# Relative-position rows of the second block: written in eight pieces from 128 partitions, in the first feed-forward

## The chip, the core and the metric

One NeuronCore of one Trainium2 chip runs the whole program. The metric is the device time of one execution in microseconds (us), as the median of three runs. Engines are named PE (TensorE), ACT (ScalarE), DVE (VectorE), POOL (GpSimd) and SP (SyncE); SP does nothing here but issue transfers.

## What is computed

Two transformer blocks run one after the other on 256 tokens of width 2048, in float32. The first block has a gated convolution, an attention with forget gates and a feed-forward of width 8192; the second has an attention with a learned relative-position bias, a pooling branch and a gated feed-forward. All that concerns the change is the bias of the second attention:

```python
dist_own = q_pos[:, None] - (own * MOBA_BLOCK + offs)[None, :]
bias_own = rel_bias[:, rel_bucket(dist_own)].astype(jnp.float32)
s_own = jnp.where(dist_own >= 0, s_own + bias_own, NEG)
```

With 256 tokens there is one block, so only this own block counts. The bias of a head depends on the distance of query and key alone: one row of 383 values per head, for distances 255 down to -127 (NEG where negative), holds everything. Query t reads that row from a start that moves by one element per query.

## The kernel before, in words

**Weights.** All large products stream their weights once. A weight tile is 512 rows by (mostly) 512 columns, 1 MB, loaded by `fetch` (line 831) as one transfer that SP issues into one of four `raw` buffers. `split_unit` (line 840) splits half a tile, a *unit*, into a high part `wh` (ACT, line 846) and a remainder `wl` (DVE, line 847), each with four buffers. `both` (line 882) then runs one *step*: six matmuls (line 887) for one 128-row slice of the weights: `wh` twice and `wl` once for each half of the tokens. A unit is two steps, a tile is four, and a chunk of 512 output columns is up to four tiles, 16 steps. The main loop (line 898) emits for each unit the split of the unit three ahead, the fetch of the tile four ahead (in the second unit of a tile), and the two steps.

**Small work.** Everything else hangs in a heap of tasks with due times counted in steps. `later(delay, fn, keys)` puts one in; after each step up to three due tasks are emitted, in the order of due time and then of insertion; `need(key)` emits tasks until the key is there. `chain` puts several in, `gap` steps apart. The order of emission is the order on each engine's own queue. `before[chunk]` runs a function ahead of a chunk's first step, after the split of the unit three ahead.

**Order of the chunks.** Values of block one (three chunks, steps 0 to 47), then queries and keys in two halves (steps 48 to 111), convolution, gates, output, and from step 464 the first feed-forward `w_ff1`: chunk j=0 is steps 464 to 479, j=1 steps 480 to 495, j=2 starts at 496. Its results are evacuated by `evac_ff` (line 559), turned by DVE transposes (line 190) into `z_t`, and split into the `k_u` operands of `w_ff2`.

**The bias.** `rel_bias_rows` (line 629) is queued for step 40. It loads a one-hot table `oh` (33x384) and the bias `rb` (33x8) on POOL's queue. A task 18 steps later multiplies them on PE into `p_b` (8x384, line 638), copies that on DVE into `e` (8 partitions, line 640) and writes `e` to DRAM 128 times over, skewed by one element per copy: one POOL transfer `ed<-e` (line 642) with 8 heads, 128 copies and 383 elements, 1532 KB. `rel_bias_tiles` (line 647) reads it back in four transfers into two `k_nb` tiles when the second block's first half of keys is done, at about 1440 us. `oh` and `e` come from the pool `s` with two buffers, which `squares` and the heads' `s_att` also use; `p_b` from the PSUM pool `tr` with four.

**What else is near step 58.** `cumulated` (line 406) writes the forget gates' sums `cd` and reads them back into two `k_nb` tiles (lines 425 and 426) on POOL's queue, `masked` (line 429) adds a mask on DVE, and two `bg` rows for the gates (line 505) stand behind the `ed` write on POOL's queue; they are first used at 330 us.

Of the kernel before, what the change touches and what calls it, by code (L numbers as in the profile page):

```python
# [11 lines left out]
F32 = mybir.dt.float32  # L12
# [7 lines left out]
P = 128  # L20
# [3 lines left out]
NH = 8  # L24
# [5 lines left out]
CW = 512  # L30
# [31 lines left out]
def tile_two_blocks(  # L62
# [5 lines left out]
    nc = tc.nc  # L68
    V, S, TE = nc.vector, nc.scalar, nc.tensor

    def pool(name, bufs, space=None):
        kw = {"space": space} if space else {}
        return ctx.enter_context(tc.tile_pool(name=name, bufs=bufs, **kw))
# [7 lines left out]
    s_p = pool("s", 2)  # L81
    pt_p = pool("pt", 3)
    bg_p = pool("bg", 2)
    st_p = pool("st", 4)
    dr_p = pool("dr", 1, DRAM)
# [7 lines left out]
    def later(delay, fn, *keys):  # L93
        seq[0] += 1
        heapq.heappush(tasks, (now[0] + delay, seq[0], fn, keys))

    def chain(delay, stages, *keys, gap=1):

        for i, fn in enumerate(stages):
            later(delay + i * gap, fn, *(keys if i == len(stages) - 1 else ()))  # L100
# [11 lines left out]
    def need(*keys):  # L112
        for key in keys:
            while key not in ready:
                run_one()
# [19 lines left out]
    chunks, before = [], {}  # L135

    def add_chunk(w, row0s, c0, ncol, acts, evac):

        chunks.append((w, row0s, c0, ncol, acts, evac))
# [7 lines left out]
    def split_out(key, j, n, p, scales=None):  # L147

        if key not in K:
            kt_tile(key)  # L150
        hi, lo = (K[key][:, h, j:j + n, :] for h in range(2))

        def to_hi():
            if scales is None:
                S.copy(hi, p)
            else:
                for i in range(n):
                    S.activation(hi[:, i, :], p[:, i, :], AF.Copy, scale=scales[i])

        def to_lo():  # L160
            if scales is None:
                V.tensor_tensor(out=lo, in0=p, in1=hi.bitcast(F32), op=OP.subtract)  # L162
            else:
                for i in range(n):
                    V.scalar_tensor_tensor(out=lo[:, i, :], in0=p[:, i, :], scalar=scales[i],
                                           in1=hi[:, i, :].bitcast(F32), op0=OP.mult, op1=OP.subtract)
        return [to_hi, to_lo]
# [12 lines left out]
    def turned(z, use, delay, keys, rate=3, lag=1):  # L180

        t = {}

        def part(i0, i1):
            if i0 == 0:
                t["o"] = z_p.tile([P, 4, T], F32, tag="z", name="z_t")
            for q, j in [divmod(i, 4) for i in range(i0, i1)]:
                src = z[32 * q:32 * q + 32].rearrange("p b (k c) -> p b k c", c=P)[:, :, :, 32 * j:32 * j + 32]
                dst = t["o"][32 * j:32 * j + 32].rearrange("p k (b t) -> p b k t", b=TB)[:, :, :, 32 * q:32 * q + 32]
                V.transpose(dst, src)  # L190

        def rest():
            for b in range(2):
                chain(lag + b, use(b, t["o"][:, 2 * b:2 * b + 2, :]), *keys[2 * b:2 * b + 2])
        n = 0
        for i in range(0, 16, rate):
            later(delay + n, lambda i=i: part(i, min(i + rate, 16)))
            n += 1
        later(delay + n - 1, rest, keys[0] + " turned")

    def group_keys(key):
        return [f"{key} {j}" for j in range(4)]
# [100 lines left out]
    AT = {}  # L303
# [233 lines left out]
    def evac_add(n, then=None):  # L537
        def evac(acc, tb=None):
            if tb is not None:
                V.tensor_tensor(out=xs[n][:, tb, :], in0=xs[n][:, tb, :], in1=acc, op=OP.add)  # L540
                nc.sync.dma_start(outr[:, tb, n * CW:(n + 1) * CW], xs[n][:, tb, :])
                return
            V.tensor_tensor(out=xs[n], in0=xs[n], in1=acc, op=OP.add)  # L543
            if then:
                then(n)
        return evac
# [12 lines left out]
    def evac_ff(key):  # L559
        def evac(acc):  # L560
            z = z_p.tile([P, TB, CW], F32, tag="z", name="z_f")
            for tb in range(TB):
                S.activation(z[:, tb, :], acc[:, tb, :], AF.Relu, scale=R["r2"][:, tb:tb + 1])
            later(1, lambda: S.activation(z, z, AF.Square))
            turned(z, lambda b, p: split_out(key, 2 * b, 2, p), 2, group_keys(key))
        return evac
# [44 lines left out]
    def k2_done(half):  # L611
        def then(z):
            y = st_p.tile([P, 8], F32, tag="hy", name="hy")
            chain(0, headnorm(z, y), f"rk{half}", gap=1)

            def scaled():
                need(f"rk{half}")
                zz = z.rearrange("p b (h d) -> p (b h) d", d=P)
                V.tensor_tensor(out=zz, in0=zz, in1=y[:, :, None].to_broadcast([P, 8, P]), op=OP.mult)
            later(5, scaled)  # L620
            transposed(z, qk_use(2, half, 1, col("kn", 0)), 8, group_keys(f"2k{half}"))
            if half == 0:
                rel_bias_tiles()
            for i in range(4):
                h = 4 * half + i
                head_task(2, h, 12 + 7 * i)
        return then

    def rel_bias_rows():
        oh = s_p.tile([33, 384], F32, tag="s", name="oh")  # L630
        nc.gpsimd.dma_start(oh, cst[0:33, C_OH:C_OH + 384])
        rb = const.tile([33, NH], F32, name="rb")
        nc.gpsimd.memset(rb[32:33, :], 1.0)
        nc.gpsimd.dma_start(rb[0:32, :], rel_bias_2.rearrange("h b -> b h"))

        def task():
            p = tr_p.tile([P, 512], F32, tag="tr", name="p_b")
            TE.matmul(p[0:8, 0:384], rb, oh, start=True, stop=True)
            e = s_p.tile([NH, 384], F32, tag="s", name="e")
            V.tensor_copy(e, p[0:8, 0:384])  # L640
            ed = dr_p.tile([NH, P * CW], F32, name="ed")
            nc.gpsimd.dma_start(bass.AP(tensor=ed.tensor, offset=ed.offset, ap=[[P * CW, NH], [CW + 1, P], [1, 383]]),
                                e[:, None, 0:383].to_broadcast([NH, P, 383]))
            AT["ed"] = ed
        later(18, task, "ed")

    def rel_bias_tiles():
        need("ed")
        ed = AT["ed"]
        for half in range(2):  # L650
            nb = k_p.tile([P, 4, MAXCOL], F32, tag="k", name="k_nb")
            o = ed.offset + half * 4 * P * CW + 127
            for c0, o, n in ((0, o + P, P), (P, o, T)):
                nc.gpsimd.dma_start(nb[:, :, c0:c0 + n],
                                    bass.AP(tensor=ed.tensor, offset=o, ap=[[CW, P], [P * CW, 4], [1, n]]))
            AT[2, "nb", half] = nb

    def v2_done(half):
# [128 lines left out]
    for blk in range(4):  # L787
        for i in range(4):
            j = 4 * blk + i
            add_chunk(w_ff1[0], G4, j * CW, CW, hT("f"), evac_ff(f"u{j}"))  # L790
        for n in range(4):
            add_chunk(w_ff2[0], [(4 * blk + i) * CW for i in range(4)], n * CW, CW, [f"u{4 * blk + i}" for i in range(4)],
                      evac_add(n, close_block if blk == 3 else None))
# [17 lines left out]
    j = 0  # L811
# [65 lines left out]
        later(4 * n + 3, lambda n=n: squares(part0, n))  # L877
    later(16, first_rstd, "r1")
    later(18, load_vectors)
    later(40, rel_bias_rows)  # L880

    def both(k, kt, wh, wl, stop):

# [77 lines left out]
```

## Time and profile before

| what | value |
|---|---|
| median of 3 runs | 2411.72 us (2409.83 to 2412.51) |
| the profiled execution | 2411.87 us |
| its span, first to last instruction | 2410.1 us |
| PE busy | 2369.9 us, 98% of the span |
| DVE busy / ACT busy | 1662.6 us (69%) / 1158.9 us (48%) |
| mean granted clock of PE | 0.995 |
| moved by DMA | 456.67 MB, mean 189 GB/s |

The profiled execution lies 1.8 us above its span and 0.15 us above the median. An engine's busy share is a mean over the whole program. PE is so near to full that its gaps can be counted one by one, so the question to ask of any other engine or transfer is in which of these gaps it ended last.

### The profile page before, as it was taken

How to read it: one execution, taken by the hardware profiler on the slowest of the kernel's cores; microseconds unless marked ns; L12 is line 12 of the kernel's file. 1: busy time of each engine (PE TensorE's matmuls, PEld its weight loads, DVE VectorE, ACT ScalarE, POOL GpSimd, SP SyncE). 2: the span in 40 equal slices, each digit the busy share in tenths (PEclk: the TensorE clock that was granted, in tenths of full speed). 3: DMA queues.
4: the chain of work that ended last, by engine and by line, in shares of the span. 5: the costliest groups of instructions: out<-in, count | busy, mean ns of one | idle time of the engine just before them, and what ended most of it. 6: DMA issues, size and time to landing. Idle time of an engine off the chain costs nothing.

```text
span 2410.1 us, 27828 instructions
## 1 busy us (share of the span) xinstructions
PE 2369.9 (98%) x10649; PEld 1962.8 (81%) x10649; DVE 1662.6 (69%) x2293; ACT 1158.9 (48%) x1514; POOL 36.5 (2%) x53
## 2 busy tenths in 40 slices
PE   9899999999999999999999999999999999999999
PEld 9688888888888888888888887888778888888877
DVE  5487776666877567577477856667787467865884
ACT  5355444444454354354345446545555345544453
POOL 1000000000000000000000000000000000000000
PEclk9899999999999999999999999999999999999999
DMA  7755565655556556555555665555555555555554
GB/s 256 188 183 171 197 207 194 210 202 176 192 179 206 192 190 195 192 192 192 192 186 181 197 209 194 161 177 190 180 181 193 192 185 182 188 194 185 185 175 140
DMA packets 230966, 456.67 MB, mean 189 GB/s; under 512 B 8085, under 2 KB 15997, under 8 KB 230832
## 3 DMA queue, kind: packets, MB, share of 16 engines
q1 hardware_dynamic: 227584, 445.81, 56.4%
q0 software_dynamic: 3248, 9.08, 1.6%
q8 instruction: 83, 1.36, 0.2%
q14 instruction: 51, 0.42, 0.0%
HBM read 451.18 MB, written 3.67 MB: 189 GB/s over the span
## 4 chain that ended last, share of the span: by engine, by line
PE 88%; DVE 6%; ACT 3%; DMA 2%; issue 1%; SPq 0%; ACTq 0%
PE acc L887 85%; DVE wl L847 2%; DVE z_t L190 2%; ACT wh L846 2%; DMA raw<-in_w_in_dram 2%; DVE z_cv L484 1%; PE p_t L175 1%; ACT z L440 1%; PE acc_last L887 0%; ACT z_cv L479 0%; PE p_t L360 0%; PE p_s L316 0%; PE p_t L714 0%; PE p_p L351 0%; DVE x L543 0%
## 5 line engine op out<-in xcount | busy, mean ns | idle before, releaser
L847 DVE TENSOR_TENSOR wl<-raw,wh 128x1024 fp32r<-128x1024 f32 (+1 forms) x848 | 1022.1, 1214 | 653.1 <-ACT wh L846 565.2
L846 ACT CAST wh<-raw 128x1024 fp32r<-128x1024 f32 (+1 forms) x848 | 874.9, 1042 | 726.3 <-PE acc L887 671.0
L887 PE MATMUL acc<-wh,k_g 128*128 128x512 f32 x1408 | 379.3, 391 | 0.0
L887 PE MATMUL acc<-wh,k_h 128*128 128x512 f32 (+1 forms) x1344 | 352.5, 384 | 12.7 <-ACT wh L846 12.7
L887 PEld LDWEIGHTS acc<-wh,k_g 128*128 128x128 f32 x1408 | 263.6, 188 | 53.9
L887 PEld LDWEIGHTS acc<-wh,k_h 128*128 128x128 f32 x1344 | 248.5, 189 | 58.5 <-ACT wh L846 14.0
L887 PE MATMUL acc<-wh,k_u 128*128 128x512 f32 x1024 | 274.8, 389 | 4.5 <-DVE k_u L162 4.5
L887 PE MATMUL acc<-wh,k_f 128*128 128x512 f32 x1024 | 273.9, 389 | 0.0
L887 PEld LDWEIGHTS acc<-wh,k_u 128*128 128x128 f32 x1024 | 191.9, 188 | 45.8 <-DVE k_u L162 6.2
L887 PEld LDWEIGHTS acc<-wh,k_f 128*128 128x128 f32 x1024 | 192.1, 188 | 39.7
L887 PE MATMUL acc<-wl,k_g 128*128 128x512 f32 x704 | 217.5, 390 | 0.0
L887 PE MATMUL acc<-wl,k_h 128*128 128x512 f32 (+1 forms) x672 | 201.4, 381 | 0.0
L887 PE MATMUL acc<-wh,k_d 128*128 128x512 f32 x656 | 176.9, 392 | 0.0
L887 PE MATMUL acc<-wl,k_f 128*128 128x512 f32 x512 | 157.6, 389 | 0.0
L887 PE MATMUL acc<-wl,k_u 128*128 128x512 f32 x512 | 157.6, 389 | 0.0
L887 PEld LDWEIGHTS acc<-wl,k_g 128*128 128x128 f32 x704 | 132.6, 188 | 27.9
L190 DVE STREAM_TRANSPOSE z_t<-z 32x256 f32<-32x256 f32 x336 | 146.4, 436 | 5.6
L887 PEld LDWEIGHTS acc<-wl,k_h 128*128 128x128 f32 x672 | 125.4, 189 | 23.2 <-DVE wl L847 0.3
L887 PEld LDWEIGHTS acc<-wh,k_d 128*128 128x128 f32 x656 | 123.2, 189 | 25.2
L887 PE MATMUL acc<-wh,k_i 128*128 128x512 f32 x512 | 140.0, 395 | 0.0
L190 DVE STREAM_TRANSPOSE z_t<-z_f 32x256 f32<-32x256 f32 x256 | 111.5, 436 | 4.1
L887 PEld LDWEIGHTS acc<-wl,k_f 128*128 128x128 f32 x512 | 96.1, 188 | 20.0
(227 smaller groups left out, 2010.3 us busy)
## 6 DMA issues: line engine op xcount, KB each, us to landing
raw<-in_w_ff_dram SPq DMA_DIRECT2D x128, 1024.0 KB, 5.2
raw<-in_w_in_dram SPq DMA_DIRECT2D x104, 1024.0 KB, 5.1
raw<-in_w_up_dram SPq DMA_DIRECT2D x88, 1024.0 KB, 5.0
raw<-in_w_down_dram SPq DMA_DIRECT2D x44, 1024.0 KB, 5.1
raw<-in_w_mix_out_dram SPq DMA_DIRECT2D x16, 1024.0 KB, 5.1
raw<-in_w_out_dram SPq DMA_DIRECT2D x16, 1024.0 KB, 5.1
raw<-in_w_conv_out_dram SPq DMA_DIRECT2D x8, 1024.0 KB, 5.3
raw<-in_w_attn_out_dram SPq DMA_DIRECT2D x8, 1024.0 KB, 5.5
```

The lines of the kernel that those rows point to most:

```text
L175: TE.transpose(p[:, j, tb * P:(tb + 1) * P], z[:, tb, (2 * b + j) * P:(2 * b + j + 1) * P], ident)
L190: V.transpose(dst, src)
L440: S.activation(z[:, tb, :], acc[:, tb, :], AF.Copy, scale=R[rname][:, tb:tb + 1])
L484: V.scalar_tensor_tensor(out=o[:, i, d:T], in0=u[:, i, 0:T - d], scalar=w(i, 2 - d), in1=o[:, i, d:T], op0=OP.mult, op1=OP.add)
L846: S.copy(wh[:, :, 0:ncol], raw)
L847: V.tensor_tensor(out=wl[:, :, 0:ncol], in0=raw, in1=wh[:, :, 0:ncol].bitcast(F32), op=OP.subtract)
L887: TE.matmul(halves[tb][:, 0:ncol], k[:, i, kt, tb * P:(tb + 1) * P], w[:, kk, 0:ncol], start=begin and first and kt == 0, stop=end and stop)
```

## The change

`rel_bias_rows` no longer runs at step 40 but ahead of the second chunk of the first feed-forward (step 480); its task follows 18 steps later. There, DVE first repeats each column of `rb` 16 times into a new tile `rbw` (33x128), so that the same matmul gives 128 rows instead of 8: 16 copies of each head's row. `e` then has 128 partitions. The one transfer on POOL's queue becomes eight on SP's, 20 steps apart from step 500 to step 640; each takes all 128 partitions and writes 128 rows of 383 elements. A head's area in DRAM is 513 elements per row in place of 512, and the addresses of the reads follow it.

```diff
-        later(18, task, "ed")
+            rbw = st_p.tile([33, NH, per], F32, tag="rbw", name="rbw", bufs=1)
+            V.tensor_copy(rbw, rb[:, :, None].to_broadcast([33, NH, per]))
             p = tr_p.tile([P, 512], F32, tag="tr", name="p_b")
-            TE.matmul(p[0:8, 0:384], rb, oh, start=True, stop=True)
-            e = s_p.tile([NH, 384], F32, tag="s", name="e")
-            V.tensor_copy(e, p[0:8, 0:384])
-            ed = dr_p.tile([NH, P * CW], F32, name="ed")
-            nc.gpsimd.dma_start(bass.AP(tensor=ed.tensor, offset=ed.offset, ap=[[P * CW, NH], [CW + 1, P], [1, 383]]),
-                                e[:, None, 0:383].to_broadcast([NH, P, 383]))
-            AT["ed"] = ed
+            TE.matmul(p[:, 0:384], rbw.rearrange("b h i -> b (h i)"), oh, start=True, stop=True)
+            e = s_p.tile([P, 384], F32, tag="s", name="e")
+            V.tensor_copy(e, p[:, 0:384])
+            ed = AT["ed"] = dr_p.tile([NH, P * ROW], F32, name="ed")
+
+            def write(k):
+                nc.sync.dma_start(bass.AP(tensor=ed.tensor, offset=ed.offset + k * ROW, ap=[[NH * ROW, P], [1, 383]]),
+                                    e[:, 0:383])
+            chain(2, [lambda k=k: write(k) for k in range(P // per)], "ed", gap=20)
+        later(18, task)
...
+            if j == 1:
+                before[len(chunks)] = rel_bias_rows
             add_chunk(w_ff1[0], G4, j * CW, CW, hT("f"), evac_ff(f"u{j}"))
...
     later(18, load_vectors)
-    later(40, rel_bias_rows)
```

`per` is 16 (128 rows over 8 heads) and `ROW` is 513; `rel_bias_tiles` uses `P * ROW` where it had `P * CW` for the stride between heads.

## Rows read from the trace of the kernel before

**Rows 1.** The page: busy time, share of the span and instructions by engine.
```profile
PE 2369.9 (98%) x10649; PEld 1962.8 (81%) x10649; DVE 1662.6 (69%) x2293; ACT 1158.9 (48%) x1514; POOL 36.5 (2%) x53
```
**Rows 2.** Who waited for whom, 70 to 140 us: total, times, longest us.
```profile
ACT k_qk L372 <- DVE z_t L190: 13.9, 2, 8.1
ACT wh L846 <- DMA raw<-in_w_in_dram: 13.7, 2, 13.0
PE acc L887 <- ACT wh L846: 11.2, 1, 11.2
```
**Rows 3.** Timeline of PE, 84 to 136 us: start, us, instruction, idle before it.
```profile
101.40 1.07 PE L887 MATMUL acc<-wh,k_h 128*128 128x512 f32 x4
...
102.76 1.07 PE L887 MATMUL acc<-wh,k_h 128*128 128x512 f32 x4
...
104.27 1.08 PE L887 MATMUL acc<-wh,k_h 128*128 128x512 f32 x4
...
116.98 2.08 PE L887 MATMUL acc<-wh,k_h 128*128 128x512 f32 x4 [11.17 <-ACT wh L846]
...
119.70 1.91 PE L887 MATMUL acc<-wh,k_h 128*128 128x512 f32 x4
...
121.93 1.09 PE L887 MATMUL acc<-wh,k_h 128*128 128x512 f32 x4
...
123.32 1.07 PE L887 MATMUL acc<-wh,k_h 128*128 128x512 f32 x4
```
**Rows 4.** Windows: length, busy by engine, granted clock (PEclk), DMA share, GB/s.
```profile
81.00:105.00 24.00, 24.00 (x107) 19.67 (x106) 16.74 (x26) 8.26 (x10) 0.00 (x0) 1.00 0.76 140
105.00:117.00 12.00, 0.83 (x5) 0.37 (x3) 0.04 (x1) 1.12 (x2) 0.00 (x0) 0.62 0.61 152
670.00:760.00 90.00, 90.00 (x398) 74.55 (x398) 69.20 (x102) 44.20 (x50) 0.00 (x0) 1.00 0.60 195
```
**Rows 5.** DMA issues, whole span: tile, queue, count, KB each, us to landing.
```profile
raw<-in_w_ff_dram SPq DMA_DIRECT2D x128, 1024.0 KB, 5.2
ed<-e POOLq DMA_DIRECT2D x1, 1532.0 KB, 37.7
out_dram<-x SPq DMA_DIRECT2D x2, 256.0 KB, 2.0
```
**Rows 6.** Timelines of POOL and SP, 60 to 140 us: when transfers were issued.
```profile
76.37 1.11 POOL L642 DMA_DIRECT2D ed<-e  x1 [2.49 <-DVE e L640]
...
80.36 0.37 SPq L837 DMA_DIRECT2D raw<-in_w_in_dram  x1
```
**Rows 7.** DMA issues in windows of 80, 95 and 125 us: that fetch, later ones.
```profile
raw<-in_w_in_dram SPq DMA_DIRECT2D x1, 1024.0 KB, 35.4
...
raw<-in_w_in_dram SPq DMA_DIRECT2D x1, 1024.0 KB, 24.7
...
raw<-in_w_in_dram SPq DMA_DIRECT2D x1, 1024.0 KB, 5.0
```
**Rows 8.** Timeline of ACT, 84 to 124 us.
```profile
102.29 0.62 ACT L372 COPY k_qk<-z_t 128x512 f32<-128x512 f32 x1
115.88 1.99 ACT L846 CAST wh<-raw 128x1024 fp32r<-128x1024 f32 x2 [12.97 <-DMA raw<-in_w_in_dram]
```
**Rows 9.** Timeline of PE, 72 to 80 us: the small matmul between two steps.
```profile
74.68 0.81 PE L638 MATMUL p_b<-oh,rb 33*8 33x384 f32 x2
```
**Rows 10.** Timelines of PE and DVE, 703 to 712 us: around step 498.
```profile
704.74 1.07 PE L887 MATMUL acc<-wh,k_f 128*128 128x512 f32 x4
...
706.10 1.07 PE L887 MATMUL acc<-wh,k_f 128*128 128x512 f32 x4
...
705.82 1.23 DVE L847 TENSOR_TENSOR wl<-raw,wh 128x1024 fp32r<-128x1024 f32 x1 [2.14 <-PE acc L887]
706.96 1.32 DVE L190 STREAM_TRANSPOSE z_t<-z_f 32x256 f32<-32x256 f32 x3
```
**Rows 11.** Groups of DVE copies by form: count, busy us, mean ns, idle before.
```profile
L640 DVE COPY e<-p_b 8x384 f32<-8x384 f32 x1 | 0.5, 545 | 1.6 <-PE p_b L638 1.6
...
L285 DVE COPY vcol<-p_v 128x160 f32<-128x160 f32 x1 | 0.3, 326 | 1.2 <-PE p_v L284 1.2
...
L412 DVE COPY c<-p_c 128x16 f32<-128x16 f32 x1 | 0.2, 168 | 0.0
```
**Rows 12.** Timelines of SP and ACT, 704 to 732 us.
```profile
707.07 0.37 SPq L837 DMA_DIRECT2D raw<-in_w_ff_dram  x1
...
722.21 1.06 ACT L846 CAST wh<-raw 128x1024 fp32r<-128x1024 f32 x1 [0.23 <-ACT wh L846]
```

More of the change, by code (lines that the diff above doesn't have):

```diff
@@ L627, in k2_done @@
         return then
+    ROW = CW + 1
     def rel_bias_rows():
@@ L634, in rel_bias_rows @@
         nc.gpsimd.dma_start(rb[0:32, :], rel_bias_2.rearrange("h b -> b h"))
+        per = P // NH
         def task():
+            rbw = st_p.tile([33, NH, per], F32, tag="rbw", name="rbw", bufs=1)
+            V.tensor_copy(rbw, rb[:, :, None].to_broadcast([33, NH, per]))
             p = tr_p.tile([P, 512], F32, tag="tr", name="p_b")
-            TE.matmul(p[0:8, 0:384], rb, oh, start=True, stop=True)
-            e = s_p.tile([NH, 384], F32, tag="s", name="e")
-            V.tensor_copy(e, p[0:8, 0:384])
-            ed = dr_p.tile([NH, P * CW], F32, name="ed")
-            nc.gpsimd.dma_start(bass.AP(tensor=ed.tensor, offset=ed.offset, ap=[[P * CW, NH], [CW + 1, P], [1, 383]]),
-                                e[:, None, 0:383].to_broadcast([NH, P, 383]))
-            AT["ed"] = ed
-        later(18, task, "ed")
+            TE.matmul(p[:, 0:384], rbw.rearrange("b h i -> b (h i)"), oh, start=True, stop=True)
[7 more added lines that the diff above has]
+        later(18, task)
     def rel_bias_tiles():
@@ L651, in rel_bias_tiles @@
             nb = k_p.tile([P, 4, MAXCOL], F32, tag="k", name="k_nb")
-            o = ed.offset + half * 4 * P * CW + 127
+            o = ed.offset + half * 4 * P * ROW + 127
             for c0, o, n in ((0, o + P, P), (P, o, T)):
                 nc.gpsimd.dma_start(nb[:, :, c0:c0 + n],
-                                    bass.AP(tensor=ed.tensor, offset=o, ap=[[CW, P], [P * CW, 4], [1, n]]))
+                                    bass.AP(tensor=ed.tensor, offset=o, ap=[[CW, P], [P * ROW, 4], [1, n]]))
             AT[2, "nb", half] = nb
```

## Prediction

> **What bounds the kernel now.** I read the page's busy times first: PE works for 98% of the span [rows 1], so what a change can win is a gap of PE or work of PE. Next come the waits and, where they are longest, PE's timeline. The waits between 70 and 140 us hold one large gap: PE stood 11.2 us for ACT's `wh`, and ACT stood 13.0 us for a weight fetch [rows 2]. In PE's timeline a step of six matmuls starts every 1.36 us (101.40 to 102.76). The next starts are 104.27, 116.98, 119.70, 121.93 and 123.32 [rows 3], so the intervals exceed 1.36 us by 0.15, 11.35, 1.36, 0.87 and 0.03: 13.76 us lost in one place. The last part of that is the clock. The granted clock was 1.00 up to 105 us and 0.62 on average in the 12 us of the gap, and the first matmuls after it ran at half pace, 2.08 us for four against 1.07 [rows 3, 4].
>
> Why the fetch was late is in the transfers. `ed<-e` was issued at 76.37 us and took 37.7 us, so it landed at 114.1 [rows 5, 6]. The fetch issued at 80.36 took 35.4 us and landed at 115.8, just when ACT resumed (115.88) [rows 6 to 8]; one issued at 96.36 still took 24.7 us, and one after `ed` had landed took 5.0 [rows 7]. A usual fetch takes 5.2 us [rows 5]. Meanwhile the DMA engines were busy 0.76 of the time at only 140 GB/s, against 0.60 at 195 in the first feed-forward [rows 4]. The skewed write held engines with slow packets, and the weights queued with it.
>
> **What the change removes.** The write leaves this place. What is late next? ACT was itself behind: it waited 8.1 us for the turned `z_t` [rows 2], and finished the second `k_qk` copy at 102.29 + 0.62 = 102.9 us [rows 8]. Without the late fetch (80.36 + 5.2 = 85.6, and even three times as slow still 96) the next `wh` runs 102.9 to 103.95 and `wl` by about 105.2. PE wants `wh` when the step that began at 104.27 ends, 105.6, and `wl` about 0.9 us later. So the unit comes in time by about a microsecond. No further transposes are due before the chunk's end, so the next splits follow at about 1.2 us each against 2.72 us of PE per unit, and the lead grows. I keep the 0.15 us before the gap as DVE's and take 13.6 us as the gain; bounds are 13.76, and 13.6 less one whole unit (2.7) if ACT and DVE come that much later than I read.
>
> PE, DVE and POOL also lose `p_b`, `e` and the issue here, and get them back at step 498. On PE the two small matmuls took 0.81 us [rows 9]; with 384 columns in both forms I take the same duration for 128 output rows, plus about 0.1 us for a wider weight load, so this move is worth +0.1 us.
>
> **What it adds on PE.** At step 498 the matmul now stands directly behind a DVE copy emitted at the same place, which the old matmul did not: it was fed by loads 18 steps old. PE would come to it at 706.10, between the second and third step of the chunk. DVE at that point is in `wl` of the unit three ahead, 705.82 to about 706.96, when its next instruction starts [rows 10]. The copy `rbw` has 128 elements on 33 partitions. Between 168 ns for 16 elements and 326 for 160 [rows 11] this is 168 + 158 x 112/144 = 0.29 us, an estimate. PE therefore waits from 706.1 to 707.3: **+1.2 us**. Bounds: 0 if `wl` runs a microsecond earlier, 2.5 if the three transposes (1.32 us) come first; by insertion order they do not. Behind the waiting matmul stand all later steps, so this is paid in full. DVE then waits for the matmul and copies `e` (128 partitions and 384 elements, 545 ns as with 8 partitions [rows 11]); its transposes and splits move by 0.3 + 0.8 + 0.5 = 1.6 us, less than PE's own 1.2 + 0.9, so nothing else becomes late.
>
> **What it adds on SP and the DMA engines.** Eight issues of 0.37 us, as one of a fetch takes [rows 6], on a queue that waits most of the time. The first one waits for `e`, until about 708.6; the fetch of 707.07 stands behind it and goes out at about 709, 2 us late, where PE is 2.1 us late too. That fetch is first needed at about 722.2 [rows 12], 15 us after its issue, and takes 5.2: a cushion of 10 us. Each piece is 191.5 KB. From below, a 256 KB store from 128 partitions landed in 2.0 us; from above, an eighth of the old write is 37.7 / 8 = 4.7 us [rows 5]. Twenty steps are 27 us with five fetches in them, at a DMA share of 0.60 [rows 4], so even 4.7 us falls in free time, and a fetch behind a piece is at most 4.7 us late, under half of the cushion. I take 0 us on the path. If the cushion were gone, it would be 2.0 to 4.7 us a piece. The store is the nearer row, since it too leaves from 128 partitions. POOL's loads of `oh` and `rb` move to step 480, 18 steps (24 us) ahead of use as before. The `s` buffer that `e` holds for 140 steps is not asked for meanwhile: nothing in the feed-forward's first half uses that pool. The read-back at 1440 us follows step 640 by some 500 us.
>
> The Trainium skill speaks against the split ("DMA: Bandwidth & Descriptors", Rules for kernel authors): transfers should be joined into 1 MiB or more, because each pays a fixed part of about 2.0 us. By that page's fit a piece would be an estimated 2.45 us and the eight 19.6 us, and paid on the path they would turn the sum into a loss of about 7 us. The trace agrees on the size (2.0 us for 256 KB) but shows such stores beside work, so I keep the rule for a rival.
>
> **The sum.** 2411.87 (profiled) - 13.6 + 1.2 + 0.1 = 2399.6; less 0.15 for the distance to the median, **2399.4 us**, a gain of 12.3 us or 0.5%.
>
> **The rivals.**
> *The gap shrinks but does not close.* The forget gates' reads and the late `z_t` remain, and with them ACT's lateness. For it: ACT's 8.1 us wait [rows 2] is no DMA's fault. Against: the next unit's sources are in place at 102.9, 2.7 us before PE runs dry. Losing one to three units' time of the gain gives 2402 to 2407, say 2404.
> *Nothing is won.* The fetches were slow for another reason (the bias rows and `k_nb` reads queued around the same time), or the time is given back later. Against: fetches recover at the moment `ed` lands, and PE at 98% has no later wait that an earlier start would lengthen. About 2412.
> *Slower: the pieces stand in the weights' way.* All eight go on SP's queue ahead of fetches. If their time is paid in line instead of hidden, 8 x 2.0 = 16 us by the store's row: 2399.4 + 16 = 2415.4; at 4.7 us each, 2437. It begins when a piece delays the following fetch by more than the 10 us cushion. Against: that is five times the store and twice an eighth of the old write. This is also where the page's rule leads.
>
> **How the numbers follow.** Forecast 0.86, shrunken gap 0.07, nothing won 0.04, slower 0.03. The forecast's own range: from 2411.7 - 13.76 + 0.1 = 2398.1 (PE waits not at all) to 2411.7 - 10.9 + 2.5 + 0.1 = 2403.4, each end with about 1 us for the spread of the runs (2.7 us from lowest to highest); the upper end lies in the rival's reach already. So 2397 to 2404. A measurement of this kernel can tell about 0.2%, 4.8 us, from no change: faster 0.92, within it 0.05, slower 0.03.
>
> **What would show it.** Right: no gap of PE over a microsecond between 80 and 130 us, granted clock 1.00 there, fetches issued after 76 us landing in 5 to 8 us; near 693 us (12 to 14 us earlier than now) one wait of PE for DVE's `rbw` of about 1.2 us; eight stores of 191.5 KB in 2 to 5 us with no wait of ACT for `raw` from 680 to 900 us. Wrong: a wait of `wh` for `raw` behind any store, a lasting PE gap near 105 us that ends with `z_t` or `k_qk`, or a second fall of the clock.

## The result

| | before | after |
|---|---|---|
| median, us | 2410.97 (2409.83 to 2412.51, 4 runs) | 2398.68 (2397.03 to 2401.46, 4 runs) |
| ratio, 95% interval | | 0.995 (0.9939 to 0.9962) |
| profiled execution, span | 2411.87, 2410.1 | 2401.46, 2399.7 |

The change saves 12.3 us, 0.5%; the 95% interval runs from 0.4% to 0.6%. The profiled execution of after is the slowest of its four runs, so the two traces differ by 10.4 us and not by 12.3. From the page of after:

```profile
PE 2369.0 (99%) x10649; PEld 1962.4 (82%) x10649; DVE 1662.5 (69%) x2294; ACT 1161.4 (48%) x1514; POOL 35.5 (1%) x52
```

PE's work is that of [rows 1] to within a microsecond; what went is time in which it stood. The place is the stretch of [rows 4]. Windows of after (length, busy by engine, clock, DMA share, GB/s):

```profile
81.00:105.00 24.00, 24.00 (x107) 19.66 (x106) 17.21 (x27) 9.98 (x12) 0.00 (x0) 1.00 0.53 186
105.00:117.00 12.00, 12.00 (x55) 9.93 (x54) 11.08 (x17) 6.77 (x8) 0.00 (x0) 1.00 0.74 264
```

From 105 to 117 us PE was busy for 0.83 us before and is busy for all 12 now, at a clock of 1.00. In the 24 us ahead of it the DMA engines move more (186 GB/s against 140) in less busy time (0.53 against 0.76). PE's timeline there answers [rows 3] (start, us, instruction):

```profile
102.02 1.07 PE L896 MATMUL acc<-wh,k_h 128*128 128x512 f32 x4
...
103.38 1.07 PE L896 MATMUL acc<-wh,k_h 128*128 128x512 f32 x4
...
104.91 1.08 PE L896 MATMUL acc<-wh,k_h 128*128 128x512 f32 x4
...
106.28 1.07 PE L896 MATMUL acc<-wh,k_h 128*128 128x512 f32 x4
```

The steps follow at 1.36, 1.53 and 1.37 us. The 0.17 us ahead of the old gap are still there; the 13.6 us of the gap are gone. What took its place in the first feed-forward, in order of time on PE, DVE and SP in the timelines of after around step 498 (answering [rows 9, 10, 12]):

```profile
691.68 1.07 PE L896 MATMUL acc<-wh,k_f 128*128 128x512 f32 x4
...
692.75 1.23 DVE L857 TENSOR_TENSOR wl<-raw,wh 128x1024 fp32r<-128x1024 f32 x1 [2.15 <-PE acc L896]
...
693.90 0.21 DVE L642 COPY rbw<-rb 33x128 f32<-33x128 f32 x1
...
694.16 0.91 PE L644 MATMUL p_b<-oh,rbw 33*128 33x384 f32 x2 [0.96 <-DVE rbw L642]
...
695.00 1.20 PE L896 MATMUL acc<-wh,k_f 128*128 128x512 f32 x4
...
695.11 0.56 DVE L646 COPY e<-p_b 128x384 f32<-128x384 f32 x1 [1.00 <-PE p_b L644]
...
695.69 0.35 SPq L650 DMA_DIRECT2D ed<-e  x1
696.14 0.39 SPq L847 DMA_DIRECT2D raw<-in_w_ff_dram  x1
...
696.50 1.09 PE L896 MATMUL acc<-wh,k_f 128*128 128x512 f32 x4
...
697.88 1.07 PE L896 MATMUL acc<-wh,k_f 128*128 128x512 f32 x4
```

PE stands 0.96 us for `rbw`, which stood behind `wl` on DVE; SP sends the first piece when `e` is there and the next fetch behind it. The pieces (median time to landing) and, from the answer on the tile `raw`, the weights' fetches of 680 to 900 us (least, median and longest time to landing):

```profile
ed<-e SPq DMA_DIRECT2D x8, 191.5 KB, 6.8
```
```profile
DMA to landing us min/median/max: 5.0/5.2/6.5
```

No fetch beside eight pieces took more than 6.5 us, and no wait of ACT for a fetch is listed between 680 and 900 us.

The 10.4 us by which the two traces differ are less than 13.6 for two reasons: the added wait, and a loss at the start, ahead of all that was changed. Windows of before and of after:

```profile
10.00:20.00 10.00, 10.00 (x64) 9.88 (x63) 7.39 (x14) 7.81 (x19) 0.00 (x0) 0.89 1.07 393
```
```profile
10.00:20.00 10.00, 9.86 (x54) 9.35 (x54) 6.61 (x12) 6.90 (x17) 0.00 (x0) 0.74 1.05 388
```

The granted clock was lower there in this execution of after, and the step after the first query chunk began at 84.34 us, though by 83.72 less the 0.97 us for the moved matmul it would have been 82.75: 1.6 us late. So 13.6 - 1.6 - 1.15 (the added wait, below) = 10.85 us, and the spans differ by 10.4. Followed step by step, the traces bear this out: after is 0.62 us late just ahead of the old gap, 12.96 us early behind it and 10.95 us early behind the moved matmul. The last half microsecond goes in small amounts, most of them after 1100 us, 0.3 us of it where PE waits for ACT's `z` near 2014 us (0.79 us where it was 0.50).

### The profile page after: what moved, and what is told of

It reads as the page before. It is cut to its first block, busy times and chain, and to the rows that moved or that the text cites. A ratio compares the mean times of both kernels' runs of the same rounds, so it can differ in the third digit from the quotient of the medians.

```text
span 2399.7 us, 27832 instructions
## 1 busy us (share of the span) xinstructions
PE 2369.0 (99%) x10649; PEld 1962.4 (82%) x10649; DVE 1662.5 (69%) x2294; ACT 1161.4 (48%) x1514; POOL 35.5 (1%) x52
## 3 DMA queue, kind: packets, MB, share of 16 engines
q8 instruction: 83, 1.36, 0.2%
## 4 chain that ended last, share of the span: by engine, by line
PE 89%; DVE 6%; ACT 3%; issue 2%; DMA 0%; SPq 0%; ACTq 0%; DVEq 0%
PE acc L896 85%; DVE wl L857 2%; DVE z_t L190 2%; DVE z_cv L484 2%; ACT wh L856 1%; PE p_t L175 1%; ACT z L440 1%; PE acc_last L896 0%; DMA x<-in_x_dram 0%; ACT z_cv L479 0%; PE p_t L360 0%; PE p_s L316 0%; PE p_t L722 0%; DVE x L543 0%; PE p_p L351 0%
## 5 line engine op out<-in xcount | busy, mean ns | idle before, releaser
L896 PEld LDWEIGHTS acc<-wl,k_u 128*128 128x128 f32 x512 | 96.1, 188 | 20.0
```

What stands on the lines that cost most here:

```text
L896: TE.matmul(halves[tb][:, 0:ncol], k[:, i, kt, tb * P:(tb + 1) * P], w[:, kk, 0:ncol], start=begin and first and kt == 0, stop=end and stop)
```

## The experiments

The change does four things to the write: another place, 128 partitions for 8, pieces, and SP's queue for POOL's. The runs take these apart. (It also moves the heads' areas in DRAM a little further apart, 513 elements per row for 512; that is answered under e10.) "Held" is how long the first fetch issued within 7 us behind the write took, where a usual one takes 5.2; "PE stood" is its longest wait for `wh` there. The list of transfers has no landing time for a store from 8 partitions on SP's queue. The times marked with a star are from its landing events in the trace, the last one less the issue (eight events behind the issue's own for each such store, sixteen for one from 16 partitions or more). Each ratio is to the runs of the kernel before that were taken with that run.

| run | partitions | pieces, queue | write landed, us | held, us | PE stood, us | median, us | ratio to before (95%) |
|---|---|---|---|---|---|---|---|
| before | 8 | 1, POOL, early | 37.7 | 35.4 | 11.2 | 2410.97 | |
| e2 | 8 | 1, POOL | 37.5 | 32.4 | 10.5 | 2410.13 | 0.9998 (0.9988 to 1.0007) |
| e6 | 8 | 1, SP | 32.0* | 34.2 | 17.1 | 2415.88 | 1.0019 (1.0009 to 1.0029) |
| e7 | 128 | 1, POOL | 9.8 | 6.5 | 0 | 2398.45 | 0.995 (0.9936 to 0.9965) |
| e3 | 128 | 1, SP | 10.1 | 11.4 | 0 | 2396.95 | 0.9948 (0.9932 to 0.9965) |
| e10 | 16 | 1, SP | 17.4 | 20.5 | 0.4 (`wl`) | 2398.74 | 0.9953 (0.9938 to 0.9968) |
| e11 | 32 | 1, SP | 11.0 | 13.6 | 0 | 2397.98 | 0.9949 (0.9929 to 0.9969) |
| e4 | 8 | 8, SP | 5.0 to 6.4* | 8.2 or less (of those listed) | 0 | 2396.79 | 0.9946 (0.9931 to 0.9961) |
| e9 | 8 | 2, SP | 16.6, 18.3* | 18.8 | 0 | 2396.42 | 0.9945 (0.9928 to 0.9961) |
| e8 | 8 | 2, POOL | 33.7 (median of 2) | 30.9 | 9.0 | 2408.18 | 0.9993 (0.9983 to 1.0002) |
| e1 | 128 | 8, SP, early | 8.5 (median) | 9.8 at most | 0 | 2397.41 | 0.9946 (0.9932 to 0.9961) |
| e5 | 128 | 8, SP | 6.6 (median) | 7.0 at most | 0 | 2395.04 | 0.9943 (0.9928 to 0.9957) |

**e2: the new place alone.** The kernel before, with only this moved:

```diff
+            if j == 1:
+                before[len(chunks)] = rel_bias_rows
...
-    later(40, rel_bias_rows)
```

> The change's new place alone: the kernel before, with the old single write from 8 partitions on POOL's queue, queued ahead of the second chunk of the first feed-forward. Theory A (the write itself holds the DMA engines, wherever it stands): it again takes about 38 us, the fetches issued in its first 10 us land when it does, and because the cushion of a fetch here is about 10 us and not 17, PE stands for 15 to 20 us near 730 us with the clock falling: 2413 to 2420 us, as slow as before or slower. Theory B (only the early place was bad, between the forget gates' reads and a late ACT): the gap goes, and the time is 2397 to 2400 us, because PE has no wait for a copy.

The gap came along. The fetch issued at 698.89 us, and ACT and PE in the timelines of this run:

```profile
raw<-in_w_ff_dram SPq DMA_DIRECT2D x1, 1024.0 KB, 32.4
```

```profile
731.37 1.99 ACT L848 CAST wh<-raw 128x1024 fp32r<-128x1024 f32 x2 [17.10 <-DMA raw<-in_w_ff_dram]
```
```profile
732.47 2.08 PE L888 MATMUL acc<-wh,k_f 128*128 128x512 f32 x4 [10.52 <-ACT wh L848]
```

Windows of the same run, at the old place and at the new one:

```profile
105.00:117.00 12.00, 12.00 (x55) 9.94 (x54) 11.02 (x19) 4.75 (x6) 0.00 (x0) 1.00 0.74 256
...
719.00:732.00 13.00, 2.96 (x14) 2.10 (x12) 0.00 (x0) 0.63 (x1) 0.00 (x0) 0.73 0.49 143
```

This is the old gap in the old size, 600 us later: a wait of ACT for a fetch, PE behind it, then four matmuls in 2.08 us at half pace. The old place was not at fault, and theory B falls. The size was less than expected (10.5 us for 15 to 20); the cushion is looked at below.

**e6 and e7: queue or partitions.** e6 is e2 with the write on SP; e7 is e3 with the write on POOL:

```diff
-            nc.gpsimd.dma_start(bass.AP(... ap=[[P * CW, NH], [CW + 1, P], [1, 383]]),
+            nc.sync.dma_start(bass.AP(... ap=[[P * CW, NH], [CW + 1, P], [1, 383]]),
```

> The old single write of 1532 KB from 8 partitions, at the new place, but issued by SP in place of POOL; with the run that has it on POOL's queue and the two with 128 partitions it makes four corners. Theory A (few partitions hold few DMA engines for long): it takes 20 to 38 us again, fetches behind it in the same queue wait for it, PE stands about 10 us: 2406 to 2412 us. Theory D (POOL's queue is what made it slow, since eight pieces from 8 partitions on SP's queue landed in 3.6 to 7.9 us, like those from 128): it lands in 10 to 18 us, no gap: 2395 to 2399 us.

> The single write of 1532 KB from 128 partitions, at the new place, issued by POOL in place of SP. Theory A (partitions): it lands in 10 to 15 us, as on SP's queue (10.1), no gap: 2395 to 2400 us. Theory D (POOL's queue): it takes 30 us or more, PE stands about 10 us: 2406 to 2412 us.

```profile
727.67 2.07 PE L888 MATMUL acc<-wh,k_f 128*128 128x512 f32 x4 [17.14 <-ACT wh L848]
```
```profile
ed<-e POOLq DMA_DIRECT2D x1, 1532.0 KB, 9.8
```

The first line is from e6's timeline of PE, the second from e7's DMA issues. The expectation of e6 takes 3.6 to 7.9 us for the landing of e4's pieces. Those are the four reads of `ed` from DRAM near 1430 us, which stand under the same name; the pieces' own times are 5.0 to 6.4 us, and the argument from them is the same. The queue doesn't decide: 128 partitions landed in 9.8 us from POOL and 10.1 from SP, and 8 partitions held the weights for over 30 us from either. Theory D falls. On SP the old write does more harm than on POOL (17.1 us for 10.5), beyond what was expected: there it goes out ahead of a fetch (692.33 us) that in e2 had left 0.8 us before the write and landed in 5.7.

**e3, e10, e11: how many partitions.** One transfer on SP's queue, from 128, 16 and 32 partitions:

```diff
-            def write(k):
-                nc.sync.dma_start(bass.AP(tensor=ed.tensor, offset=ed.offset + k * ROW, ap=[[NH * ROW, P], [1, 383]]),
-                                    e[:, 0:383])
-            chain(2, [lambda k=k: write(k) for k in range(P // per)], "ed", gap=20)
+            def write():
+                nc.sync.dma_start(bass.AP(tensor=ed.tensor, offset=ed.offset,
+                                          ap=[[NH * ROW, P], [ROW, NH], [1, 383]]),
+                                  e[:, None, 0:383].to_broadcast([P, NH, 383]))
+            later(2, write, "ed")
```

For 16 and 32 `per` is 2 and 4, and each partition is written 64 and 32 times.

> 128 partitions, but one transfer of 1532 KB on SP's queue at step 500 in place of eight pieces. Theory A (few partitions make the write slow; pieces matter little): a piece landed in 3.4 us at its fastest, so the whole takes at most 8 x 3.4 = 27 us and by the bytes of a fetch (1024 KB in 5.2 us) 8 us; the fetch behind it is late by 8 to 20 us against a cushion of 10, so PE stands for 0 to 10 us: 2398 to 2411 us, likeliest 2399. Theory C (the size of one transfer is what holds the weights up, whatever its partitions): it takes about 38 us again and PE stands 15 to 20 us: 2413 to 2420 us.

> One write of 1532 KB on SP's queue from 16 partitions, each written 64 times, two copies of each head's row. If the number of source partitions sets the time in proportion (8 partitions held the fetch behind them 34.2 us, 128 partitions 11.4), 16 partitions lie near the 8: about 17 to 20 us if twice the partitions are twice as fast, PE stands 0 to 2 us: 2396 to 2401 us. If 8 is a limit of its own (so many DMA engines in use) and 16 is already enough for all, it lands in 10 to 12 us, no wait: 2395 to 2399 us. The Trainium skill (DMA: Bandwidth & Descriptors, Rules for kernel authors, on using all 16 engines) says that an outermost dimension below 16 confines a transfer to that many engines, and so expects the second.

> The same from 32 partitions. If the time falls in proportion to the partitions, it lands in about 9 to 10 us, half of that of 16; if 16 are already enough, 16, 32 and 128 land alike, in 10 to 12 us. In either case no gap: 2395 to 2399 us.

The DMA issues of e3, e10 and e11:

```profile
ed<-e SPq DMA_DIRECT2D x1, 1532.0 KB, 10.1
```
```profile
ed<-e SPq DMA_DIRECT2D x1, 1532.0 KB, 17.4
```
```profile
ed<-e SPq DMA_DIRECT2D x1, 1532.0 KB, 11.0
```

Eight pieces are not needed: the whole from 128 partitions in one transfer leaves PE no gap. In the packet records of the traces the rows of the write, 1532 bytes each, go out over 30.8 us in e6 (8 partitions), 15.5 in e10, 7.9 in e11 and 6.2 in e3: 51, 101, 199 and 253 GB/s. The rate doubles with the partitions up to 32, and then hardly grows. So the first expectation for 16, in proportion, is the one that came about (17.4 us to landing for 17 to 20, and 0.4 us of PE's time); for 32 the rows keep the proportion (7.9 us) and the landing does not (11.0 us for 9 to 10), as it counts the 1.3 us before the first row and the time behind the last too.

A row took 0.214 us at the median in e6 and 0.215 in e10, 219 us in all in both: from 8 to 16 partitions no row got faster, and twice as many were under way (7 and 14 at a time). From 16 to 32 as many were under way (14 to 15), and the row itself got faster, 0.108 us; from 128 it took 0.069.

The Trainium skill ("DMA: Bandwidth & Descriptors", Rules for kernel authors, on using all 16 engines) says that an outermost dimension below 16 confines a transfer to at most that many engines. The first halving agrees with it; that 16 would then be as good as 128 does not follow, 17.4 us against 10.1, and the second halving, with hardly more rows under way, can't be put down to more engines. The distance of the heads' areas is not the cause either: e6 has the old one and e10 the new, and their rows take the same time.

**e4: eight pieces from 8 partitions.** e2 with the write cut, on SP:

```diff
+            def write(k):
+                nc.sync.dma_start(bass.AP(tensor=ed.tensor, offset=ed.offset + k * per * (CW + 1),
+                                          ap=[[P * CW, NH], [CW + 1, per], [1, 383]]),
+                                  e[:, None, 0:383].to_broadcast([NH, per, 383]))
+            chain(2, [lambda k=k: write(k) for k in range(NH)], "ed", gap=20)
```

> Eight pieces, 20 steps apart on SP's queue in the first feed-forward, but each from the old 8 partitions (16 copies of each head's row), with the old matmul to 8 rows and no widened table. Theory A (the cost of a write is that of its 8 partitions, and it hurts only beyond the cushion): each piece takes an eighth of 37.7 us, 5 to 8 us behind a fetch, under the cushion of 10 us: no gap, and no wait of PE for the widened table, 2397 to 2399 us. If the 128 partitions are what brings the gain, the pieces still delay fetches and PE stands behind some of them: 2401 to 2411 us.

The pieces in e4's DMA issues, without a time to landing; by their landing events they took 5.0 us (the first) to 6.4:

```profile
ed<-e SPq DMA_DIRECT2D x8, 191.5 KB
```

No gap, 2396.79 us: pieces alone suffice as well, without a widened table and PE's wait for it. So either half of the change's recipe closes the gap, and the two together close it no further. The pieces are not harmless by faster rows alone: those of the first piece, which had no fetch directly ahead, took 0.215 us at the median, as long as in the whole write, but there were only 128 of them.

**e8 and e9: two halves.** e2 with two transfers of 766 KB, 40 steps apart in the order of emission, on POOL and then on SP:

```diff
+            def write(k):
+                nc.gpsimd.dma_start(bass.AP(tensor=ed.tensor, offset=ed.offset + k * 64 * (CW + 1),
+                                            ap=[[P * CW, NH], [CW + 1, 64], [1, 383]]),
+                                    e[:, None, 0:383].to_broadcast([NH, 64, 383]))
+            chain(0, [lambda k=k: write(k) for k in range(2)], "ed", gap=40)
```

> The old write from 8 partitions on POOL's queue at the new place, in two halves of 766 KB, 40 steps (54 us) apart. If a write does harm only by what it takes beyond the weights' cushion: each half takes about 19 us; a fetch issued just after it lands when it does, 17 to 20 us later; ACT, which wanted its weights 15.4 us after the fetch when the whole write stood here, waits 0 to 4 us, and PE, which ran on for 7.7 us after ACT stood, not at all: 2395 to 2399 us. If any such write costs PE in proportion, each half costs about 5 us and the sum stays that of before, 2407 to 2411 us.

> The old write from 8 partitions in two halves of 766 KB, 40 steps apart, now on SP's queue, where the fetches that stand between them keep them apart (on POOL's queue nothing stood between them and they went out 0.8 us apart). If a write does harm only beyond the cushion: the whole on SP's queue held the fetch behind it for 34.2 us, so a half holds it for about 18; ACT wanted that fetch 12.6 us after its issue and PE stood 18.2 us after it, so ACT waits 3 to 6 us and PE 0 to 2 us: 2395 to 2400 us. If the harm is in proportion, two halves cost as much as the whole, 2410 to 2416 us.

POOL's timeline in e8, and ACT's in e9:

```profile
693.14 1.66 POOL L644 DMA_DIRECT2D ed<-e  x2 [42.52 <-DVE e L640]
```
```profile
712.09 1.05 ACT L851 CAST wh<-raw 128x1024 fp32r<-128x1024 f32 x1 [4.41 <-DMA raw<-in_w_ff_dram]
```

e8 did not test what it was meant to. Both halves went out within 1.66 us: a step is a place in the order of emission, and POOL's queue held nothing between the two that would make it wait. They acted as one write, and PE stood 9.0 us. On SP's queue (e9) ten fetches stand between the halves, each waiting for its buffer, and they came 50 us apart. A half held the fetch behind it for 18.8 us, ACT waited 4.4 us, and PE not at all. Harm begins beyond a cushion and is not in proportion to the bytes.

**e1: the pieces at the old place.** The changed kernel, queued at step 40 again, with pieces two steps apart:

```diff
-            chain(2, [lambda k=k: write(k) for k in range(P // per)], "ed", gap=20)
+            chain(2, [lambda k=k: write(k) for k in range(P // per)], "ed", gap=2)
...
+    later(40, rel_bias_rows)
```

> The changed kernel's pieces from 128 partitions, but at the old place: queued at step 40, written from step 60 on, two steps apart. Theory A (the form of the write alone closes the gap, wherever it stands): eight pieces of 3.4 to 7 us within 22 us delay the fetches by a few us each, under the cushion; no gap of PE between 80 and 130 us, one wait of about 1 us for the widened table, now near 75 us: 2395 to 2400 us, as the changed kernel. Theory B (the place between the forget gates' reads and a late ACT counts too): the gap returns in part, 2402 to 2410 us.

No gap, 2397.41 us: the place needn't change. The wait for `rbw` that was expected near 75 us isn't there; DVE had come to the copy in time, and only the 0.4 us of PE's own last products stand ahead of the weight load.

**e5: the widened table five steps earlier.**

```diff
-            rbw = st_p.tile([33, NH, per], F32, tag="rbw", name="rbw", bufs=1)
-            V.tensor_copy(rbw, rb[:, :, None].to_broadcast([33, NH, per]))
+            rbw = AT["rbw"]
...
+        def widen():
+            rbw = AT["rbw"] = st_p.tile([33, NH, per], F32, tag="rbw", name="rbw", bufs=1)
+            V.tensor_copy(rbw, rb[:, :, None].to_broadcast([33, NH, per]))
+        later(13, widen)
         later(18, task)
```

> The changed kernel with the copy of the widened table emitted five steps ahead of the matmul. If PE's 1.0 us at the matmul (its weight load 1.4 us) is a wait for DVE's queue at that point, it goes to under 0.3 us, and the step that spans the matmul loses 2.1 us less 1.1: 2397.5 us, 1.1 us less than the changed kernel, within what the comparison can tell; the trace decides. If the wait is for something else (the loads of the one-hot table, ACT), it stays.

PE's timeline in e5:

```profile
690.18 1.07 PE L900 MATMUL acc<-wh,k_f 128*128 128x512 f32 x4
...
691.63 0.91 PE L643 MATMUL p_b<-oh,rbw 33*128 33x384 f32 x2
692.47 1.19 PE L900 MATMUL acc<-wh,k_f 128*128 128x512 f32 x4
...
693.96 1.09 PE L900 MATMUL acc<-wh,k_f 128*128 128x512 f32 x4
...
695.34 1.07 PE L900 MATMUL acc<-wh,k_f 128*128 128x512 f32 x4
```

The wait is gone. The three intervals exceed 1.36 us by 0.93, 0.13 and 0.02, 1.08 us in all, where they did by 2.12 in the changed kernel (steps at 691.68, 695.00, 696.50 and 697.88 us): 1.04 us less. The median of 2395.04 is the lowest of all, but its range (2394.86 to 2398.71) overlaps that of the changed kernel, so that by the times alone the two can't be told apart.

## Why the prediction was right, point by point

**The gap and its cause: shown.** Its 13.6 us are gone from the trace, and e2 moved them along with the write. The prediction named the write's slow packets as the cause without saying which of its properties made them slow; e2, e6, e3 and e7 show that it is the few partitions, on either queue, and e10 and e11 that the rate follows their number up to 32.

**What is late next: right.** ACT's casts, which the prediction put at 102.9 us, came at 103.45, in a trace that ran 0.6 us later there; `wl` followed at 104.53, and PE lost 0.17 us, as it did before.

**PE's wait for `rbw`: right in place, a little high.** Predicted 1.2 us and 0.1 for the wider load; the steps there lost 2.12 us against 0.97 around the old matmul, so 1.15 more. The copy took 0.21 us where two other copies gave 0.29. The 0.1 us for the wider load, which the prediction took from no row, is there: a weight load took 184 ns for 128 rows and 84 for 8, and in e5, without the wait, the steps lost 1.08 us, 0.11 more than the old 0.97. The old 0.97 is what these steps of before take beyond 1.36 us each (2.19, 1.50 and 1.36 us):

```profile
73.23 1.07 PE L887 MATMUL acc<-wh,k_h 128*128 128x512 f32 x4
...
75.42 1.19 PE L887 MATMUL acc<-wh,k_h 128*128 128x512 f32 x4
...
76.92 1.07 PE L887 MATMUL acc<-wh,k_h 128*128 128x512 f32 x4
...
78.28 1.07 PE L887 MATMUL acc<-wh,k_h 128*128 128x512 f32 x4
```

**Eight pieces on SP: right that they cost nothing, wrong in their size.** The range was 2.0 to 4.7 us to landing; the fastest took 3.4 and the median 6.8. The rows chosen for the bounds were a store with nothing ahead of it and an eighth of the old write. What counts is the fetch of 1 MB that had just gone out on the same queue: seven of eight pieces were issued right behind one (for instance 0.4 us, at 885.82 after 885.40) and waited for it: their first rows moved 3.9 to 4.1 us after the issue. The first, with none directly ahead, moved after 0.9 us and is the 3.4. The fetches behind pieces took 6.5 us at most, so that the rival in which pieces hold up weights, and with it the Trainium skill's rule of joining transfers ("DMA: Bandwidth & Descriptors", Rules for kernel authors), did not come about. The fit of that page is given there for transfers that GpSimd issues (Anatomy of one DMA), and the pieces went on SP's queue; by it the store of 256 KB would be an estimated 2.6 us, and it took 2.0. For this kernel the rule's advice would have done as well (e3: one transfer, 10.1 us), as long as it leaves from enough partitions.

**The cushion: too small.** The prediction counted 10 us: 15 until ACT wants the weights, less 5.2. But ACT works three units ahead of PE, and what it waits is not yet PE's. In e2 the fetch of 698.89 us was wanted by ACT at 714.3 (15.4 us later) and PE stood at 721.9 (23 us); in e6 it was 12.6 and 18.2; in e10, with a fetch of 20.5 us, PE's longest wait for weights was 0.4. So a fetch may take some 18 to 23 us in the feed-forward before PE stands, 13 to 18 over its usual time. The old write overran that; a half of it (18.8 us) did not.

**The sum.** 13.6 less 1.15 is 12.45 us, the medians give 12.3; that the terms' small errors are 0.1 us in the end is luck, as the spread of the runs is 4 us.

## What to carry to other kernels

Look for a small transfer that lands late beside a stream that lands late: a write from 8 partitions held the weights for 35 us, the same bytes from 128 partitions for 7 to 11. Spread its source over more partitions or cut it so that each piece fits the stream's cushion; either is enough, and moving it is not. Pieces keep their distance only on a queue that has something between them to wait for.

## What the runs showed of the hardware that was not expected

- One transfer of 1532 KB to DRAM, rows of 1532 bytes: from 8 partitions 37.5 us on POOL's queue and 32.0 on SP's, from 16 partitions 17.4, from 32 partitions 11.0, from 128 partitions 10.1 on SP's and 9.8 on POOL's. On SP's queue, beside the weights, the rows moved at 51, 101, 199 and 253 GB/s: in proportion to the partitions up to 32. The row's time stayed between 8 and 16 (0.214 and 0.215 us) and halved at 32 (0.108); why was not tried.
- Cut in eight (e4), rows from 8 partitions took 0.065 us at the median in the seven pieces that stood behind a fetch, and 0.215 in the first, which did not. So they are not slow only when many are queued: 128 rows are enough. In the second half of e9, issued 0.4 us behind a fetch, the first 64 rows took 0.065 us at the median and the later ones 0.21 to 0.22. Why the first rows behind a fetch are short stays open.
- After PE had stood 10.5 us in e2, four matmuls took 2.08 us where they take 1.07 at the granted clock of 1.00: the lower of the two clock levels, as after the old gap [rows 3]. In e10, with no wait for weights over 0.4 us, the clock stayed at 1.00.
